# One bias tile with one-hot selectors, a new load order, and idle products at the planner's early gaps

## The chip, the cores and the metric

The kernel runs on one core of one Trainium2 chip. The metric is the device time of one execution in microseconds. A kernel's time is the median of its runs; a profiled execution is a run of its own, with its own time and a span (first to last instruction) that is a little shorter than that time.

## What is computed

The reference is one layer of an encoder trunk: 256 rows of 2048 values, all in 32-bit floats. A conditioning vector c gives six vectors of 2048 (shift, scale and gate for each of two sub-layers). The first sub-layer is windowed attention with 32 query heads and 8 key heads, the second a squared-ReLU MLP with 8192 hidden values:

```
mod = silu(c) @ mod_w + mod_b              # 2048 x 12288
sh_m, sc_m, g_m, sh_f, sc_f, g_f = split(mod, 6)
h = x * (1 + sc_m) + sh_m
y = attention(h @ w_qkv + b_qkv) @ w_o + b_o
x = layer_norm(alpha * x + (1 + g_m) * y)
h = x * (1 + sc_f) + sh_f
y = square(relu(h @ w1 + b1)) @ w2 + b2
out = layer_norm(alpha * x + (1 + g_f) * y)
```

Nearly all of the bytes are weights, each of which is read once: 288.54 MB in the profiled execution.

## The kernel before

**Split products.** TensorE (PE) multiplies in a reduced 32-bit form, so each operand is split into a high and a low part and a product is done as three: high by high, high by low, low by high (`mm3`, lines 893 to 898, which shows as L894, L895, L896). ScalarE (ACT) casts the high half of a weight (`Stream.half`, L614), and VectorE (DVE) subtracts it from the raw weight to get the low half (`Stream.low`, L572). One load is a raw tile of 128 x 2048 floats, 1 MB, and gives two halves of 128 x 1024. There are five high and five low half tiles, and eight raw tiles while the planned part lasts (five after it). All of these loads go out on the queue of SyncE (SP), in the order of one list, as raw tiles come free.

**Modulation.** The shift and scale of each 128-row chunk of the input come in one of two forms, chosen by `MIXP` (line 33): as a product on PE (`Mod.step`, L679; then a copy on ACT at L707, a product that turns it at L769, and an addition on DVE at L776), or as two columns on DVE (`Col.step`, L718), each of which multiplies a whole raw tile by the conditioning vector and sums it. Six of the 16 chunks are products. The column form needs the vector in all 128 partitions (`cb`); it is spread there by PE (`spread`, L972, whose stationary operand is one column read 128 times) and copied by ACT. The modulated input is then made on ACT (L924, L927) and DVE (L929). The first gate is four loads on PE and twelve columns on DVE.

**The gate row.** `Gate.spread` (line 810) turns the gate columns into a row: an addition on DVE (s1, L814), a product on PE (s2, L817), a copy on ACT and a store to DRAM from the queue of GpSimd (POOL) (s3, L820 and L821), and a read of that row into all 128 partitions, also from POOL's queue (s4, L824). The sums that use it are three operations on DVE for each column block and row tile: a product (tm, L1342), an addition (za, L1344), statistics (bn, L1346).

**The biases.** `bias_rows` (line 487) is called twice, for the attention's input bias (six rows of 512) and its output bias (four rows). Each call makes four tiles of 128 x 1024: the rows at partition 0 and 32, their split into a high and a low part, and a table of selectors in which each row of ones is written out 128 wide. ACT copies the selectors (L502), DVE splits the rows (L504, L505), and `add` (L508) multiplies a selector by the split rows to add one row to a bank.

**The order of the work.** From the start to about the eleventh weight of the MLP every engine's order is fixed by a planner, `flow_order` (line 122). `FLOW` (line 64) is the list of loads: "m" a modulation chunk (two loads), a number or a pair a weight of the attention's input product, "g" and "G" the gate's columns and products, "f" a column for the second modulation, "x" the rows of the input, ("o", c, j) a weight of the output product for column block c, "F" a weight of the MLP. `COST` (line 76) holds the planned duration of each kind of operation. The planner steps through time, takes for each engine what is ready, with ranks for ties, counts PSUM banks and raw tiles, and sorts all operations by planned start. The kernel then issues them in that order, and the helper `P` ties each instruction to the one before it on its engine, so an instruction that waits holds up all that stand behind it on its engine. After the planned part the MLP runs in four blocks in plain loops (L1503, L1505 and `mm3`).

**Idle products.** `idle(n)` (line 1005) issues n products of 128 x 512 into a bank that nobody reads, to keep PE's clock up. Before has 12 at the very start, 5 and 2 ahead of and between the first chunk's products, 8 behind its turn, and 18 ahead of the first layer norm.

Of the kernel before, what the change touches and what calls it, by code (L numbers as in the profile page):

```python
# [19 lines left out]
D = 2048  # L20
# [12 lines left out]
MIXP = tuple(int(k in (0, 1, 2, 4, 6, 15)) for k in range(16))  # L33
# [14 lines left out]
def mod_chunks():  # L48
# [8 lines left out]
    for which, p in (("m", GMP), ("f", 0)):  # L57
# [21 lines left out]
            s3=.2, s4=6.0, wm=1.4, v1=.3, v2=.25, v3=.43, n0=.46, n1=.74, fr=.3, fx=.4, fk=.45,  # L79
            fy=.6, ft=.82, fa=.46, fb=.46, fc=.36, w=1.44, ev=.5, ed=.6, i0=1.2, i1=.9, i2=.6, i3=.5, i4=.45, sv=1.0, sa=.96)  # L80
# [41 lines left out]
def flow_order():  # L122
# [4 lines left out]
    def op(key, eng, kind, after, rank, banks=(), frees=(), slot=False):  # L127
        ops[key] = eng, kind, list(after), rank, banks, frees, slot

    weights = [v[1] for v in loads if v[0] == "w"]  # L130
    tiles = max(i for i, v in enumerate(loads) if v[0] == "m")
    early = [v[1] for v in loads[:tiles] if v[0] == "w"]
    for k in range(NK):
        g0, g1 = ("g", k, 0), ("g", k, 1)
        if MIXP[k]:
            op(g0, "PE", "gP", [("m", k, 0)], 0, ("gv",) if k == 0 else (), (), True)
            op(g1, "PE", "gP", [("m", k, 1), g0], 0, (), (), True)
            op(("r", k), "ACT", "r", [g1], 0)
            op(("c", k), "PE", "c", [("r", k)], 0)
            op(("a", k), "DVE", "a", [("c", k)], 0, (), ("gv",) if not any(MIXP[k + 1:]) else ())  # L140
        else:
            for i, g in enumerate((g0, g1)):
                op(g, "DVE", "gD", [("m", k, i), ("cp", 3)], 2, (), (), True)
            op(("a", k), "DVE", "a", [g0, g1], 0)
        op(("H", k), "ACT", "H", [("a", k)], 0)
        op(("T", k), "ACT", "H", [("a", k)], 1)
        op(("S", k), "DVE", "S", [("H", k), ("T", k)], 0)
# [3 lines left out]
    for n in weights:  # L151
# [14 lines left out]
        for i in range(4):  # L166
# [37 lines left out]
            if kind == "u" and k == NK - 1 or kind == "l" and n[0] == 3 and i == 3:  # L204
                p = p if kind == "u" else n[1]
                op(("bq", p), "PE", "bq", [("u", n, i), ("sv", 0), ("sa", 0)], 1)
# [24 lines left out]
    for x in range(2):  # L231
        op(("sv", x), "DVE", "sv", [("i", 4)], 4)
        op(("sa", x), "ACT", "sa", [("i", 4)], 4)
# [132 lines left out]
    return [key for _, _, key in sorted(out)], loads  # L366
# [6 lines left out]
def hybrid_kernel(ctx: ExitStack, tc: tile.TileContext, a, out: bass.AP):  # L373
# [25 lines left out]
    def g4(dt=F32):  # L399
        return gen.tile([128, 1024], dt, tag="g4", name="g4")  # L400
# [86 lines left out]
    def bias_rows(src, n):  # L487


        m = n // 512  # L490
        raw, hl, one, sel = g4(), g4(F32R)[:, :512], g4(), g4(F32R)
        nc.gpsimd.memset(raw[:, :512], 0.0)
        nc.gpsimd.memset(one, 0.0)
        v = one[:, :m * 128].rearrange("p (m n) -> p m n", m=m)
        for p in (0, 32):
            nc.gpsimd.dma_start(raw[p:p + m, :512], src.rearrange("o (m n) -> (o m) n", m=m))
            nc.gpsimd.affine_select(out=v, in_=v, compare_op=OP.not_equal, fill=1.0, base=-p,
                                    pattern=[[-1, m], [0, 128]], channel_multiplier=1)

        def split(sels):  # L500
            if sels:
                P(nc.scalar.copy(sel, one))  # L502
            else:
                P(nc.vector.tensor_copy(hl, raw[:, :512]))  # L504
                P(nc.vector.tensor_sub(hl[32:32 + m], raw[32:32 + m, :512], f32(hl[32:32 + m])))  # L505

        def add(ps, c, stop=True):
            P(nc.tensor.matmul(ps, sel[:, c * 128:c * 128 + 128], hl, start=False, stop=stop))  # L508

        return split, add  # L510
# [330 lines left out]
    KEYS, LOADS = flow_order()  # L841
# [457 lines left out]
    split_bias, bq = bias_rows(a["bqkv"], QKV)  # L1299
    split_bo, bo = bias_rows(a["bo"], D)  # L1300
# [33 lines left out]
    def row_bias(c):  # L1334
        for t in range(NT):
            bo(out_of[c][0][t], c, False)
# [10 lines left out]

    for key in KEYS:
        op, *v = key
        if op == "g":  # L1350
            k, i = v
            S.take(load_of["m", k, i])
            if k == 0:
                idle((5, 2)[i])
# [8 lines left out]
        elif op == "c":  # L1363
            m_mix[v[0]].turned()
            if v[0] == 0:
                idle(8)
# [6 lines left out]
        elif op in ("sv", "sa"):  # L1373
            (split_bo if v[0] else split_bias)(op == "sa")
# [354 lines left out]
```

## Time and profile before

| what | before |
|---|---|
| median of 3 runs | 1078.09 us (1076.59 to 1078.45) |
| profiled execution | 1077.52 us |
| its span | 1075.7 us |
| PE busy | 1047.2 us, 97% |
| DVE busy | 821.4 us, 76% |
| ACT busy | 538.2 us, 50% |
| POOL busy | 22.3 us, 2% |
| moved by DMA | 291.63 MB, mean 271 GB/s |
| granted TensorE clock | 0.990 of full |

A line of a profile names the line of the kernel, the engine, the operation and the tiles as out<-in. Lines with "x" and a number group instructions. What stands in brackets at the end of a timeline's line is the time for which the engine had no work just before, and what ended that. PE's busy time is modelled (matmuls are pipelined), so a stop shows in the brackets, and a low clock shows only in the stretches' column of the granted clock. DVE and the DMA engines are the ones to watch up to about 420 us, PE alone behind that.

### The profile page before, as it was taken

The numbers are of one execution on the slowest core, as the hardware profiler recorded it, in microseconds if no ns is written. First come the engines' busy times: TensorE is split into PE (matmuls) and PEld (weight loads), VectorE is DVE, ScalarE is ACT, GpSimd is POOL, SyncE is SP. The second block draws the span as 40 slices with busy tenths as digits, with TensorE's granted clock in tenths as the row PEclk, the third lists the DMA queues.
The fourth block names the chain that finished last, engine by engine and source line by source line (L and its number), as shares of the span: only waits on it lengthen the run. The fifth ranks groups of instructions, "written<-read, shape, count | busy, mean of one in ns | idle before, by whom it ended". The sixth has DMA issues, their size and how long they took to land.

```text
span 1075.7 us, 15033 instructions
## 1 busy us (share of the span) xinstructions
PE 1047.2 (97%) x5896; PEld 875.8 (81%) x5896; DVE 821.4 (76%) x1139; ACT 538.2 (50%) x833; POOL 22.3 (2%) x45
## 2 busy tenths in 40 slices
PE   7999999999988999999999999999999999999997
PEld 5787776677767999988888888888888888888885
DVE  2679999899979999955787879656665557665795
ACT  3545359899414655733445543344543334554340
POOL 3000000000000000000000010000000000000000
PEclk8999999999989999999999999999999999999999
DMA  9999997668977998655778788756555555557522
GB/s 380 425 426 425 427 423 299 223 214 313 422 302 304 337 423 307 220 192 193 267 278 293 270 293 328 302 209 220 181 187 196 196 196 196 193 180 257 192 78 79
DMA packets 43463, 291.63 MB, mean 271 GB/s; under 512 B 4940, under 2 KB 5100, under 8 KB 9600
## 3 DMA queue, kind: packets, MB, share of 16 engines
q1 hardware_dynamic: 40256, 281.82, 69.1%
q0 software_dynamic: 2272, 7.40, 2.1%
q10 hardware_dynamic: 864, 1.45, 0.4%
q8 instruction: 46, 0.75, 0.3%
q14 instruction: 25, 0.20, 0.0%
HBM read 288.54 MB, written 2.11 MB: 270 GB/s over the span
## 4 chain that ended last, share of the span: by engine, by line
PE 76%; DVE 17%; ACT 3%; DMA 3%; issue 1%; SPq 0%; DVEq 0%; POOLq 0%; ACTq 0%
PE pa L1503 16%; PE pa L894 13%; PE pa L896 13%; PE pa L895 13%; PE pa L1505 9%; DVE raw L718 6%; DVE wl L572 5%; PE pa L1285 2%; PE pa L1283 2%; PE pa L1284 2%; DMA raw<-in_wqkv 1%; ACT g L1105 1%; PE pt L1111 1%; PE pa L1065 1%; DMA g<-rowm 1%
## 5 line engine op out<-in xcount | busy, mean ns | idle before, releaser
L572 DVE TENSOR_TENSOR wl<-raw,wh 128x1024 fp32r<-128x1024 f32 x332 | 402.1, 1222 | 191.6 <-ACT wh L603 175.6
L603 ACT CAST wh<-raw 128x1024 fp32r<-128x1024 f32 x226 | 237.9, 1053 | 317.6 <-PE pa L896 181.1
L894 PE MATMUL pa<-wh,g 128*128 128x512 f32 x816 | 323.8, 397 | 4.9 <-ACT wh L614 2.3
L895 PE MATMUL pa<-wl,g 128*128 128x512 f32 x816 | 320.8, 393 | 5.1 <-DVE wl L572 5.1
L896 PE MATMUL pa<-wh,g 128*128 128x512 f32 x816 | 320.4, 393 | 0.1
L1503 PE MATMUL pa<-g,wh 128*128 128x512 f32 x768 | 192.3, 392 | 0.0
L718 DVE CUSTOM_DVE_ANT_0 raw<-raw,cb 128x2048 f32<-128x2048 f32 x80 | 182.0, 2284 | 8.7 <-DMA raw<-in_mod 8.7
L894 PEld LDWEIGHTS pa<-wh,g 128*128 128x128 f32 x816 | 154.7, 190 | 40.7 <-issue 2.9
L895 PEld LDWEIGHTS pa<-wl,g 128*128 128x128 f32 x816 | 154.7, 190 | 37.4 <-DVE wl L572 6.6
L896 PEld LDWEIGHTS pa<-wh,g 128*128 128x128 f32 x816 | 154.7, 190 | 33.3 <-DVE g L929 0.7
L1503 PEld LDWEIGHTS pa<-g,wh 128*128 128x128 f32 x768 | 138.3, 189 | 25.1 <-ACT wh L603 0.2
L614 ACT CAST wh<-raw 128x1024 fp32r<-128x1024 f32 x106 | 109.1, 1051 | 95.4 <-PE pa L896 38.5
L1505 PEld LDWEIGHTS pa<-g,wl 128*128 128x128 f32 x768 | 104.8, 190 | 7.5
L1505 PE MATMUL pa<-g,wl 128*128 128x256 f32 x768 | 107.1, 282 | 0.0
L1284 PE MATMUL pa<-g,wh 128*128 128x256 f32 x256 | 72.5, 284 | 0.9 <-DVE g L1259 0.9
L1283 PE MATMUL pa<-g,wh 128*128 128x256 f32 x256 | 72.7, 285 | 0.6 <-DVE g L1293 0.3
L1285 PE MATMUL pa<-g,wl 128*128 128x256 f32 x256 | 72.5, 283 | 0.6 <-DVE wl L572 0.6
L1284 PEld LDWEIGHTS pa<-g,wh 128*128 128x128 f32 x256 | 49.1, 192 | 1.4 <-DVE g L1259 1.4
L1283 PEld LDWEIGHTS pa<-g,wh 128*128 128x128 f32 x256 | 48.9, 192 | 1.1 <-ACT g L1261 0.5
L1285 PEld LDWEIGHTS pa<-g,wl 128*128 128x128 f32 x256 | 49.1, 192 | 0.8 <-DVE wl L572 0.8
L1082 ACT ACTIVATE g<-g,nm 128x256 f32<-128x256 f32 x64 | 32.0, 508 | 0.9 <-DVE nm L1074 0.8
L1074 DVE CUSTOM_DVE_ANT_0 g<-pa,msk,nsnk 128x256 f32<-128x256 f32 x64 | 27.1, 476 | 2.0 <-PE pt L1111 1.1
(194 smaller groups left out, 703.9 us busy)
## 6 DMA issues: line engine op xcount, KB each, us to landing
raw<-in_mod SPq DMA_DIRECT2D x96, 1024.0 KB, 8.0
raw<-in_w SPq DMA_DIRECT2D x64, 1024.0 KB, 4.9
raw<-in_w1b SPq DMA_DIRECT2D x48, 1024.0 KB, 4.8
raw<-in_wqkv SPq DMA_DIRECT2D x24, 1024.0 KB, 10.8
raw<-in_wo SPq DMA_DIRECT2D x16, 1024.0 KB, 7.7
raw<-in_w1a SPq DMA_DIRECT2D x16, 1024.0 KB, 7.1
g<-in_x SPq DMA_DIRECT2D x4, 512.0 KB, 11.7
gb<-in_lnrow POOLq DMA_DIRECT2D x8, 256.0 KB, 5.6
```

What stands on the lines that cost most here:

```text
L572: self.pinned(nc.vector.tensor_sub(l, r, f32(self.hs[n])))
L603: self.last[n] = nc.scalar.copy(h, s)
L614: self.pinned(nc.scalar.copy(h, s))
L718: S.pinned(nc.vector.tensor_tensor_reduce(out=raw, in0=raw, in1=cb, scale=1.0, scalar=0.0, op0=OP.mult, op1=OP.add, accum_out=self.dst))
L894: S.pinned(nc.tensor.matmul(ps, xh, wh, start=start, stop=False))
L895: S.pinned(nc.tensor.matmul(ps, xh, wl, start=False, stop=False))
L896: S.prev = nc.tensor.matmul(ps, xl, wh, start=False, stop=stop)
L1283: S.pinned(nc.tensor.matmul(o, wh(w, 128), hh, start=new and fi + k == 0, stop=False))
L1284: S.pinned(nc.tensor.matmul(o, wh(w, 128), hl, start=False, stop=False))
L1285: S.pinned(nc.tensor.matmul(o, wl(w, 128), hh, start=False, stop=end and fi == 1 and k == 3))
L1503: nc.tensor.matmul(ps, wh(k, 128), ff_in(k), start=k == 0, stop=False)
L1505: nc.tensor.matmul(ps[:, :256], wl(k, 128), ff_in(k)[:, :256], start=False, stop=k == NK - 1)
```

## The change

Three things are changed, all in the planned part.

1. `bias_rows` is called once, with both biases. Their ten rows share one tile (at partitions 0 to 9 and again from 32 on). The selector of a row is one column of a small tile of 128 x 10, and `add` reads that column 128 times as its stationary operand. The split is one step on DVE (a copy of the small tile, then copy and subtraction of the rows); ACT has no part in it.
2. `FLOW` and `MIXP` are replaced. The product form goes to the chunks 0, 1, 2, 3, 10, 14 instead of 0, 1, 2, 4, 6, 15. The counts of all kinds of load are the same. In `COST`, s4 (the gate row's way back) is 15.0 instead of 6.0, and the two splits (sv, sa) become one sv of 1.2. The first product of a product-form chunk is planned behind the addition of the product-form chunk ahead of it.
3. The planner also returns `FILL`: for each operation of PE, how many idle products fit the gap that it plans ahead of it, at 0.3 us each. The kernel issues them as long as no spread and no weight of the pair form has come yet; the calls with 5, 2 and 8 are gone.

```
-MIXP = tuple(int(k in (0, 1, 2, 4, 6, 15)) for k in range(16))
+MIXP = tuple(int(k in (0, 1, 2, 3, 10, 14)) for k in range(16))
 FLOW = [
-    "m", "m", 0, 1, "m", 2, "m", "m", (0, 4), 3, (0, 3), (0, 5), "m", 4, "m", (1, 4), "m", "m", 5, (1, 3), "m", 6,
-    "m", (1, 5), 7, "m", (2, 3), 8, "m", (2, 5), 9, "m", 10, "m", "m", 11, "g", (3, 3), "f", "G", "f", (2, 4),
-    (3, 4), "G", (3, 5), "x", "g", "g", ("o", 0, 0), ("o", 0, 1), "g", ("o", 1, 1), "G", "f", ("o", 1, 2), "g", "g",
-    "f", "f", ("o", 0, 2), "g", ("o", 1, 0), "g", "g", "G", "g", "f", ("o", 1, 3), ("o", 0, 3), "f", "g", "g",
-    ("o", 2, 0), ("o", 3, 1), "f", ("o", 2, 2), "f", "f", ("o", 3, 0), "f", "f", ("o", 2, 3), ("o", 2, 1), "f", "f",
-    "f", "f", "f", ("o", 3, 3), ("o", 3, 2), "f", "f", "f", "f", "F", "F", "f", "F", "F", "f", "f", "F", "f", "F",
-    "F", "f", "f", "F", "f", "f", "f", "f", "F", "F", "F", "f", "F", "F",
+    "m", 0, "m", 1, "m", 2, (0, 5), "m", "m", (0, 3), "m", 3, "m", (0, 4), 4, (1, 5), "m", (1, 4), 5, "m", 6, "m",
+    (1, 3), 7, (2, 5), "m", "m", 8, (2, 3), "m", 9, "m", "m", 10, "m", 11, "g", (3, 3), "g", "G", "G", (2, 4),
+    (3, 4), "g", (3, 5), "g", ("o", 1, 0), "g", "g", "f", ("o", 0, 1), "f", "g", "f", "x", ("o", 1, 1), ("o", 0, 0),
+    "G", "f", "G", "g", "g", ("o", 1, 2), "f", "g", "g", "g", ("o", 0, 2), ("o", 1, 3), ("o", 0, 3), "f", "f",
+    ("o", 3, 3), ("o", 2, 1), ("o", 2, 3), "f", "f", "f", ("o", 3, 1), "f", "f", "f", ("o", 3, 2), "f", ("o", 3, 0),
+    "f", "f", "f", ("o", 2, 0), ("o", 2, 2), "f", "f", "f", "f", "F", "F", "f", "f", "F", "f", "F", "F", "f", "f",
+    "f", "F", "F", "f", "f", "f", "F", "f", "f", "F", "F", "F", "F", "F",
 ]
...
-            s3=.2, s4=6.0, wm=1.4, v1=.3, v2=.25, v3=.43, n0=.46, n1=.74, fr=.3, fx=.4, fk=.45,
+            s3=.2, s4=15.0, wm=1.4, v1=.3, v2=.25, v3=.43, n0=.46, n1=.74, fr=.3, fx=.4, fk=.45,
...
-            op(g0, "PE", "gP", [("m", k, 0)], 0, ("gv",) if k == 0 else (), (), True)
+            op(g0, "PE", "gP", [("m", k, 0)] + rowed, 0, () if rowed else ("gv",), (), True)
+            rowed = [("a", k)]
...
+    keys, fill, end = [], {}, 0.0
+    for t, _, key in sorted(out):
+        keys.append(key)
+        if ops[key][0] == "PE":
+            fill[key] = max(int((t - end - .2) / .3), 0) if end else 0
+            end = t + COST[ops[key][1]]
+    return keys, loads, fill
...
+    def bias_rows(srcs):
+
+        raw, hl = g4()[:, :512], g4(F32R)[:, :512]
+        m = [n // 512 for _, n in srcs]
+        one, pick = cst.tile([128, sum(m)], F32, name="one"), cst.tile([128, sum(m)], F32R, name="pick")
...
+        def split():
+            e = 32 + sum(m)
+            P(nc.vector.tensor_copy(pick, one))
+            P(nc.vector.tensor_copy(hl, raw))
+            P(nc.vector.tensor_sub(hl[32:e], raw[32:e], f32(hl[32:e])))
 
         def add(ps, c, stop=True):
-            P(nc.tensor.matmul(ps, sel[:, c * 128:c * 128 + 128], hl, start=False, stop=stop))
+            P(nc.tensor.matmul(ps, pick[:, c:c + 1].to_broadcast([128, 128]), hl, start=False, stop=stop))
...
+    free = True
     for key in KEYS:
         op, *v = key
+        free = free and op != "sp" and (op != "u" or type(v[0]) is int)
+        if free and FILL.get(key):
+            idle(FILL[key])
         if op == "g":
             k, i = v
             S.take(load_of["m", k, i])
-            if k == 0:
-                idle((5, 2)[i])
```

More of the change, by code (lines that the diff above doesn't have):

```diff
@@ L78 @@
             no=.4, pt=.43, pc=.48, va=1.9, oh=.48, ol=.6, tm=.6, za=.6, bn=.6, mr=.2, mt=.15, ma=.1, s1=.1, s2=.35,
-            s3=.2, s4=6.0, wm=1.4, v1=.3, v2=.25, v3=.43, n0=.46, n1=.74, fr=.3, fx=.4, fk=.45,
-            fy=.6, ft=.82, fa=.46, fb=.46, fc=.36, w=1.44, ev=.5, ed=.6, i0=1.2, i1=.9, i2=.6, i3=.5, i4=.45, sv=1.0, sa=.96)
+            s3=.2, s4=15.0, wm=1.4, v1=.3, v2=.25, v3=.43, n0=.46, n1=.74, fr=.3, fx=.4, fk=.45,
+            fy=.6, ft=.82, fa=.46, fb=.46, fc=.36, w=1.44, ev=.5, ed=.6, i0=1.2, i1=.9, i2=.6, i3=.5, i4=.45, sv=1.2)
 AFTER = dict(PE=.35, DVE=.2, ACT=.2, Q=0.0)
@@ L131, in flow_order @@
     tiles = max(i for i, v in enumerate(loads) if v[0] == "m")
+    rowed = []
     early = [v[1] for v in loads[:tiles] if v[0] == "w"]
@@ L205, in flow_order @@
                 p = p if kind == "u" else n[1]
-                op(("bq", p), "PE", "bq", [("u", n, i), ("sv", 0), ("sa", 0)], 1)
+                op(("bq", p), "PE", "bq", [("u", n, i), ("sv",)], 1)
                 d = done.setdefault(CORD[p], [])
@@ L215, in flow_order @@
             if out_of[c] == 0:
-                op(("bo", c), "PE", "bq", [("u", n, 3), ("sv", 1), ("sa", 1)], 3)
+                op(("bo", c), "PE", "bq", [("u", n, 3), ("sv",)], 3)
             out_of[c] += 1
@@ L230, in flow_order @@
         op(("i", x), "ACT" if x == 3 else "DVE", "i%d" % x, [("i", x - 1) if x else ("u", weights[0], 3)], 4)
-    for x in range(2):
-        op(("sv", x), "DVE", "sv", [("i", 4)], 4)
-        op(("sa", x), "ACT", "sa", [("i", 4)], 4)
+    op(("sv",), "DVE", "sv", [("i", 4)], 4)
     for v in loads:
@@ L365, in flow_order @@
         out.append((t, len(out), key))
-    return [key for _, _, key in sorted(out)], loads
+    keys, fill, end = [], {}, 0.0
[5 more added lines that the diff above has]
+    return keys, loads, fill
 ORDER_ONLY = mybir.DependencyInfo(mybir.DependencyClass.NoSync, mybir.DependencyReason.DATA)
@@ L484, in rotary_tables @@
         yield
[L487 to L492, printed above, removed]
+    def bias_rows(srcs):
+        raw, hl = g4()[:, :512], g4(F32R)[:, :512]
+        m = [n // 512 for _, n in srcs]
+        one, pick = cst.tile([128, sum(m)], F32, name="one"), cst.tile([128, sum(m)], F32R, name="pick")
+        nc.gpsimd.memset(raw, 0.0)
         nc.gpsimd.memset(one, 0.0)
-        v = one[:, :m * 128].rearrange("p (m n) -> p m n", m=m)
         for p in (0, 32):
[L496 to L505, printed above, removed]
+            for (src, _), i, k in zip(srcs, (0, m[0]), m):
+                nc.gpsimd.dma_start(raw[p + i:p + i + k], src.rearrange("o (m n) -> (o m) n", m=k))
+            nc.gpsimd.affine_select(out=one, in_=one, compare_op=OP.not_equal, fill=1.0, base=-p,
+                                    pattern=[[-1, sum(m)]], channel_multiplier=1)
+        def split():
[3 more added lines that the diff above has]
+            P(nc.vector.tensor_sub(hl[32:e], raw[32:e], f32(hl[32:e])))
         def add(ps, c, stop=True):
-            P(nc.tensor.matmul(ps, sel[:, c * 128:c * 128 + 128], hl, start=False, stop=stop))
+            P(nc.tensor.matmul(ps, pick[:, c:c + 1].to_broadcast([128, 128]), hl, start=False, stop=stop))
         return split, add
@@ L839, in hybrid_kernel @@
     m_gf = Gate("f", 0, gateb[:, 1])
-    KEYS, LOADS = flow_order()
+    KEYS, LOADS, FILL = flow_order()
     load_of = {}
@@ L1298, in hybrid_kernel @@
     load_x(0)
-    split_bias, bq = bias_rows(a["bqkv"], QKV)
-    split_bo, bo = bias_rows(a["bo"], D)
+    split_bias, bq = bias_rows(((a["bqkv"], QKV), (a["bo"], D)))
     msk = masks()
@@ L1335, in row_bias @@
         for t in range(NT):
-            bo(out_of[c][0][t], c, False)
+            bq(out_of[c][0][t], QKV // 512 + c, False)
     def gated_sum(op, c, t):
@@ L1364, in hybrid_kernel @@
             m_mix[v[0]].turned()
-            if v[0] == 0:
-                idle(8)
         elif op == "a":
@@ L1372, in hybrid_kernel @@
             next(rotary)
-        elif op in ("sv", "sa"):
-            (split_bo if v[0] else split_bias)(op == "sa")
+        elif op == "sv":
+            split_bias()
         elif op == "h":
```

## The prediction

> **What bounds the kernel now.** I read the page first, then stretches of the span, then the waits, then the chain and the timeline around the longest wait.
>
> ```profile
> span 1075.7 us, 15033 instructions
> ...
> L572 DVE TENSOR_TENSOR wl<-raw,wh 128x1024 fp32r<-128x1024 f32 x332 | 402.1, 1222 | 191.6 <-ACT wh L603 175.6
> ...
> L718 DVE CUSTOM_DVE_ANT_0 raw<-raw,cb 128x2048 f32<-128x2048 f32 x80 | 182.0, 2284 | 8.7 <-DMA raw<-in_mod 8.7
> ```
>
> The profiled execution took 1077.52 us, 1.8 us more than its span; the median of the three runs is 1078.09, that is 0.57 us more than this execution. L572 makes the low half of a weight (1.22 us for each 128x1024 half); L718 makes one column of the modulation from one load (2.28 us). Both run on VectorE (DVE) and follow the planner's order. Next, chosen stretches; the columns are the stretch and its length, busy time and count of TensorE (PE), of its weight loads, of DVE, ScalarE (ACT) and GpSimd (POOL), then the granted clock, the DMA share and GB/s.
>
> ```profile
> 19.00:26.00 7.00, 6.32 (x16) 4.76 (x17) 5.06 (x5) 3.93 (x6) 0.00 (x0) 0.52 1.03 434
> 46.20:50.00 3.80, 3.73 (x9) 2.56 (x10) 2.50 (x4) 3.80 (x6) 0.00 (x0) 0.55 1.01 425
> 80.00:140.00 60.00, 58.48 (x256) 47.40 (x255) 59.77 (x69) 27.69 (x34) 0.00 (x0) 1.00 1.01 426
> 160.00:260.00 100.00, 96.19 (x657) 67.60 (x656) 94.49 (x241) 93.10 (x259) 0.00 (x0) 1.00 0.67 254
> 296.00:304.00 8.00, 7.89 (x35) 6.19 (x33) 2.73 (x5) 2.41 (x3) 0.00 (x0) 1.00 1.01 422
> 303.90:307.80 3.90, 0.01 (x1) 0.01 (x1) 3.83 (x7) 0.85 (x1) 0.00 (x0) 0.77 0.15 63
> 307.80:312.80 5.00, 5.00 (x12) 3.94 (x13) 5.00 (x6) 0.00 (x0) 0.00 (x0) 0.50 0.79 279
> 320.00:340.00 20.00, 20.00 (x90) 16.56 (x89) 19.86 (x23) 4.88 (x5) 0.00 (x0) 1.00 0.98 396
> 460.00:1040.00 580.00, 580.00 (x2913) 493.95 (x2912) 392.96 (x462) 259.04 (x310) 8.01 (x15) 1.00 0.64 227
> ```
>
> From 460 to 1040 us PE has no free time and no other engine is near full. The diff leaves that stretch as it is, so whatever the planned part (up to some 420 us) gains or loses goes to the end one for one. In the planned part there are several limits: the DMA engines and DVE both full from 80 to 140, PE, DVE and ACT all over 93% from 160 to 260. The weak place is at 296 to 313: DVE works 2.73 of 8 us, then PE stands for 3.9 us, and then PE has half its clock for 5 us. The waits of DVE say why; the columns are the total, the number of times and the longest.
>
> ```profile
> DVE tmp L1342 <- DMA g<-rowm: 5.8, 1, 5.8
> DVE modm L776 <- PE gv L769: 5.4, 3, 4.7
> ```
>
> The chain and DVE's timeline show the way of the gate row: from the copy on ACT, through DRAM and back in 128 copies, to the first product with it.
>
> ```profile
> 286.88 0.26 ACT grow L820
> ...
> 287.42 5.19 DMA rowm<-grow
> ...
> 293.19 7.98 DMA g<-rowm
> ```
>
> ```profile
> 295.31 0.08 DVE L718 DVE_READ_ACCUMULATOR2_ANT modf<- 128x1 f32 x1
> 301.20 0.69 DVE L1342 TENSOR_TENSOR tmp<-pa,g 128x512 f32<-128x512 f32 x1 [5.80 <-DMA g<-rowm]
> ...
> 306.52 4.62 DVE L572 TENSOR_TENSOR wl<-raw,wh 128x1024 fp32r<-128x1024 f32 x4
> ```
>
> From the end of the copy (287.14) to the first product that uses the row (301.20) it is 14.06 us. The planner of before counts 6.0 for this (s4), and so puts the products eight microseconds too early in DVE's queue. Behind them stand four halves of weights (306.52), and PE runs dry at 303.9 because they are late.
>
> **The change, part by part.**
>
> *The gate row at 15 (s4).* Planned at 15, the products of L1342 stand behind 15 us of other DVE work, 0.9 us more than the way took. Low halves and columns are there to fill it: the load list has three output weights behind the last gate column, and modulation loads after them. PE needs no bank from these products meanwhile: four column blocks of the output product take eight banks, and before had already begun its third block ahead of them. The order search also puts the last gate column at load 82 instead of 87, five loads earlier. What PE loses here now is 3.90 us standing and 5.00 us at clock 0.50, so 3.9 + 2.5 = 6.4 us; what DVE loses is 5.80. From 320 to 340 DVE is busy 19.86 of 20, so PE cannot gain more than DVE gives: I take 5.8, with ends 0 (the wait comes elsewhere) and 6.4.
>
> Here the Trainium skill speaks against the change. "DMA: Bandwidth & Descriptors", section "Anatomy of one DMA — SWDGE (gpsimd) path", fits a GpSimd-issued DMA as 2.0 us plus its bytes at 436 GB/s; for the row of 8 KB and then 1 MB this estimate is 2.0 + 4.4 = 6.4 us, which would make the old 6.0 right, leave nothing to gain in this term, and put the sum at 1075.1 instead of 1069.3 for the profiled execution. The rows differ from it: 5.19 and 7.98 us, with the other loads holding the DMA engines at a share of 1.01. The wait of 5.80 is measured, so the rows decide.
>
> *The load order of the first 52 loads and the forms (MIXP).* Product form on PE stays at six of 16 chunks, so DVE keeps 20 column loads of 2.28 us and the DMA engines the same bytes. Three product chunks move: 4, 6 and 15 become columns, 3, 10 and 14 products. The first weight now comes after one modulation chunk, not two. PE's early losses are here:
>
> ```profile
> 19.16 0.74 PE L894 MATMUL pa<-wh,g 128*128 128x512 f32 x1 [2.28 <-ACT wh L614]
> ...
> 46.14 0.50 PE L894 MATMUL pa<-wh,g 128*128 128x512 f32 x1 [1.79 <-ACT g L924]
> ...
> 150.40 0.62 PE L508 MATMUL pa<-g,g 128*128 128x512 f32 x2
> ```
>
> Two stops of 2.28 and 1.79 us, each followed by a cold stretch (7.0 us at 0.52 costs 3.4, 3.8 at 0.55 costs 1.7): 9.2 us in all. Not all of it can come back. The DMA engines must bring 52 loads of 1.049 MB and 2.1 MB of the input, 56.6 MB, at 426 GB/s: 133 us; half a cast, 1.2 us of low half and 24 products at 0.222 us (90 in 20 us) then end no earlier than about 141, against 150.40 for the bias product that follows the last chunk. That room is more than DVE can use, which is full from 80 to 140 (59.77 of 60). What DVE visibly wastes ahead of that is the one wait of 4.7 us for a product-form chunk queued behind weights on PE (chunk 6, now a column). I take half of it, 2.4 us, because another chunk may come late instead; ends 0 and 5.8 (the 4.7 and the bias work below), and a loss is the rival below.
>
> *Idle products.* Before has 5, 2 and 8 of them at the first chunk; now the planner's gaps are filled, 0.3 us counted for each where a warm one takes 0.222 and a cold one twice that. A gap of 3 us gets nine, which take 2.0 us warm and 4.0 us cold, so a cold fill can end 1.0 us late. They stop at the first spread of the conditioning vector or the first quarter, so the stop at 44 us is not of the kind that they cover. PE waits for loads there anyway: 0, ends minus 1 and plus 1 us.
>
> *One bias tile.* Removed: one split on DVE and both ACT copies of selectors; added: a copy of 10 columns.
>
> ```profile
> L972 PEld LDWEIGHTS pa<-ident,cact x32: 185/190/333, 24.9 to 32.8; 128*128 128x128 f32 x32
> ```
>
> ```profile
> L508 PEld LDWEIGHTS pa<-g,g x20: 186/188/192, 150.2 to 300.3; 128*128 128x128 f32 x20
> ```
>
> ```profile
> 41.78 0.43 DVE L504 CAST g<-g 128x512 fp32r<-128x512 f32 x1
> 42.25 0.68 DVE L505 TENSOR_TENSOR g<-g,g 4x512 fp32r<-4x512 f32 x1
> ```
>
> DVE saves 1.1 us less one small copy, near 42 us, where it is not full; it is inside the end of 5.8 above and counts 0 alone. The selector is now one column read 128 times, as L972 already loads its weight: 190 ns against 188 for the stored selector, over 20 products, 0. POOL's DMAs stay four and its fills get smaller, all before 10 us: 0. The input rows (x) load nine places later; they are first used behind the products with the gate row: 0. With more tiles free and the row of gv waited for by name, no wait is added that before did not have.
>
> *The rest of the order (160 to 420 us).* The same operations in a new sequence. DVE's idle time from 160 to 260 is 5.5 us; taking a third of it away, or adding as much, gives ends of minus 2 and plus 2. Later, the eighth weight of the next layer moves from load 123 to 126: three loads at 2.46 us, 7.4 us of lead lost where DMA is nearly full; at worst a stop of about 2 us and a cold stretch like that after 46 us, 1.7: plus 4. I take 0.
>
> **Sum:** 1077.52 - 5.8 - 2.4 = 1069.3 for the profiled execution; with 0.57 for the median, 1069.9 us.
>
> **The rivals.**
>
> *Gate row alone.* The start stays bound by the DMA engines (share 1.01 from 80 to 140) and gives nothing: 1078.09 - 5.8 = 1072.3. For it: PE and DVE both trail the loads. Against it: the 4.7 us wait.
>
> *The wait returns.* The row's way runs beside the loads; DVE no longer stalls, so raw tiles are freed and loads press on. Each microsecond beyond 15 is again a wait of DVE, and at 20.8 the 5.8 are back; if the start gives nothing either, 1076 to 1078. Against it: the share was 1.01 already while the row was under way. This is also the case in which the change doesn't do what it says.
>
> *Slower: the last modulation chunk as a column.* Chunk 15 was a product, and is now two columns at loads 50 and 51, just ahead of the last weight.
>
> ```profile
> 119.42 7.82 SPq L556 DMA_DIRECT2D raw<-in_mod  x4
> ```
>
> ```profile
> 138.56 2.28 DVE L718 CUSTOM_DVE_ANT_0 raw<-raw,cb 128x2048 f32<-128x2048 f32 x1
> ...
> 144.42 0.43 DVE L929 TENSOR_TENSOR g<-xm,g 128x256 fp32r<-128x256 f32 x1 [1.16 <-ACT xm L927]
> ```
>
> ```profile
> raw<-in_mod SPq DMA_DIRECT2D x4, 1024.0 KB, 8.7
> ```
>
> Chunk 14's first load was issued at 119.42 and landed 8.7 us later, at 128.1; DVE took it at 138.56, 10.4 us behind. Chunk 15 lands two loads (4.9 us) later, 133.0. With the same backlog: 143.4, two columns to 148.0, 1.7 for the rest as from 143.1 to 144.85, then 18 products (4.0) to 153.7: 3.3 us later than 150.40. PE has nothing else meanwhile, since the next chunk needs the same columns, and starts cold: 2.5 as after 307.8. Plus 5.8 is just the gate row's gain, so 10.4 us of backlog is where it decides; at 14 the total is 1078.1 + 3.6 = 1081.7. Against it: chunks 10 and 14 are now products, which gives DVE four loads (9.8 us) without columns, where before had none between loads 23 and 49.
>
> **How the numbers follow.** Forecast 0.48; gate row alone 0.22; wait returns 0.15; last chunk late 0.15. About 0.2% (2.2 us) is what a measurement of this kernel can tell from no change. The first two are faster, with 0.02 of the third: 0.72; the third otherwise the same: 0.13; the fourth slower: 0.15. The range reaches down by the upper ends (6.4, 5.8 and 2 from 1078.1: 1063.9, rounded to 1063.5) and up to 1077.5, which leaves out the slower rival and the worst of the third.
>
> **What would show it.** Right: no wait of DVE on g<-rowm over 1 us; no stop of PE over 1.5 us and no cold stretch between 160 and the layer norm; the output product's last chunk 5 to 9 us earlier; the bias product of the first stage at 147 to 149. Wrong: the bias product after 151 with a stop ahead of it; DVE again idle on the row; a new stop with a clock near 0.5 in the next layer's first weights; or a stretch from 460 to 1040 that is not full.

## The result and the profile after

| | before | after |
|---|---|---|
| median, runs side by side | 1077.34 us (4 runs, 1076.42 to 1078.45) | 1064.96 us (4 runs, 1064.95 to 1066.41) |
| ratio, 95% interval | 1 | 0.9888 [0.9871, 0.9905] |
| profiled execution, its span | 1077.52, 1075.7 us | 1064.97, 1063.2 us |

The kernel is 12.4 us faster. The page of after, its first lines:

```profile
span 1063.2 us, 15010 instructions
...
PE 1042.3 (98%) x5894; PEld 873.4 (82%) x5894; DVE 820.2 (77%) x1138; ACT 535.5 (50%) x831; POOL 17.4 (2%) x41
```

PE has 4.9 us less busy time than the 1047.2 of before (PE at half clock is busy for longer with the same work); the other 7.6 us of the span were free time of PE. To place them I cut the span at four instructions that both kernels have. The rows of a source line give a group's durations, then its first and last start; before, then after:

```profile
L1130 PE MATMUL pa<-g,g x128: 379/379/431, 181.8 to 271.6; 128*64 128x256 f32 x128
...
L1247 PE MATMUL pt<-ident,g x32: 270/295/476, 344.9 to 388.3; 128*128 128x128 f32 x32
...
L1503 PE MATMUL pa<-g,wh x768: 389/389/497, 535.0 to 976.5; 128*128 128x512 f32 x192
```

```profile
L513 PEld LDWEIGHTS pa<-g,pick x20: 185/188/192, 144.8 to 291.6; 128*128 128x128 f32 x20
L513 PE MATMUL pa<-g,pick x20: 390/397/501, 145.1 to 291.8; 128*128 128x512 f32 x20
...
L1135 PE MATMUL pa<-g,g x128: 379/379/430, 173.9 to 264.3; 128*64 128x256 f32 x128
...
L1252 PE MATMUL pt<-ident,g x32: 272/273/421, 330.1 to 371.2; 128*128 128x128 f32 x32
...
L1507 PE MATMUL pa<-g,wh x768: 389/389/497, 522.4 to 963.9; 128*128 128x512 f32 x192
```

**Start** runs up to the first bias product (150.4 before, by the prediction's row; 145.1 after), **attention** from there to the last product with the values (L1130, now L1135), **gate row** from there to the first transpose behind the layer norm (L1247, now L1252), **MLP start** from there to the first product of the plain loops (L1503, now L1507). The change of each: start -5.3, attention -2.0 (121.2 to 119.2), gate row -7.5 (73.3 to 65.8), MLP start +2.3 (190.0 to 192.3); together -12.5, the whole change of the span. The same stretches as in the prediction, for after (times shifted with the work):

```profile
19.00:26.00 7.00, 6.00 (x63) 4.86 (x62) 4.24 (x11) 4.06 (x6) 0.00 (x0) 1.00 1.02 425
46.20:50.00 3.80, 3.03 (x13) 2.17 (x12) 3.80 (x5) 2.27 (x4) 0.00 (x0) 1.00 1.03 425
100.00:140.00 40.00, 40.00 (x272) 32.20 (x265) 33.67 (x41) 15.40 (x22) 0.00 (x0) 1.00 1.01 421
160.00:260.00 100.00, 99.03 (x651) 72.36 (x650) 98.63 (x249) 97.29 (x270) 0.00 (x0) 1.00 0.80 298
287.00:303.00 16.00, 16.00 (x72) 13.17 (x72) 15.86 (x19) 5.27 (x5) 0.00 (x0) 1.00 0.98 390
386.00:388.40 2.40, 1.01 (x6) 0.81 (x7) 1.79 (x3) 1.89 (x3) 0.00 (x0) 0.99 1.01 423
388.40:391.80 3.40, 3.40 (x18) 3.40 (x18) 3.40 (x5) 2.68 (x3) 0.00 (x0) 0.50 0.83 296
447.00:1027.00 580.00, 580.00 (x2913) 493.95 (x2912) 392.55 (x462) 259.47 (x310) 7.99 (x15) 1.00 0.64 227
```

The clock is 1.00 where before had 0.52 and 0.55. In the attention PE is busy 99.03 of 100 instead of 96.19. Through the sums with the gate row (287 to 303) PE never stops. In the plain loops PE's figures are unchanged to the hundredth. New is a weak place at 386. The waits of DVE, and its timeline with POOL's and ACT's around the row:

```profile
DVE modm L781 <- PE gv L774: 10.4, 3, 5.0
DVE raw L723 <- DMA raw<-in_mod: 8.4, 6, 3.6
```

```profile
270.68 0.26 ACT L825 COPY grow<-pt 16x128 f32<-16x128 f32 x1 [0.63 <-PE pt L822]
...
277.29 1.09 POOL L829 DMA_DIRECT2D g<-rowm  x2 [5.54 <-DMA rowm<-grow]
...
286.39 0.68 DVE L1346 TENSOR_TENSOR tmp<-pa,g 128x512 f32<-128x512 f32 x1
...
385.54 1.99 ACT L619 CAST wh<-raw 128x1024 fp32r<-128x1024 f32 x2 [6.27 <-DMA raw<-in_w1a]
...
386.63 0.39 PE L1288 MATMUL pa<-g,wh 128*128 128x256 f32 x1 [0.73 <-ACT wh L619]
...
387.89 0.38 PE L1290 MATMUL pa<-g,wl 128*128 128x256 f32 x1 [0.75 <-DVE wl L577]
```

No wait on g<-rowm is left: the first product with the row has no bracket, 15.45 us after ACT's copy ended (286.39 less 270.94). At 386 ACT stands 6.27 us for the load of the ninth MLP weight, PE stops twice for 0.7 us and then works at half clock. The wait for product-form chunks (modm<-gv), of which I meant to win half, has grown from 5.4 to 10.4 us; that for column loads (8.4) is what it was (8.7).

### The profile page after: what moved, and what is told of

It reads as the page before. It is cut to its first block, busy times and chain, and to the rows that moved or that the text cites. A ratio compares the mean times of both kernels' runs of the same rounds, so it can differ in the third digit from the quotient of the medians.

```text
span 1063.2 us, 15010 instructions
## 1 busy us (share of the span) xinstructions
PE 1042.3 (98%) x5894; PEld 873.4 (82%) x5894; DVE 820.2 (77%) x1138; ACT 535.5 (50%) x831; POOL 17.4 (2%) x41
## 4 chain that ended last, share of the span: by engine, by line
PE 70%; DVE 18%; DMA 8%; issue 2%; ACT 1%; DVEq 0%; ACTq 0%; SPq 0%
PE pa L1507 17%; PE pa L899 13%; PE pa L900 13%; PE pa L901 13%; PE pa L1509 9%; DVE raw L723 7%; DVE wl L577 5%; DMA raw<-in_mod 3%; DVE g L1079 2%; DMA raw<-in_wqkv 2%; PE pa L1289 2%; PE pa L1290 2%; PE pa L1288 2%; DMA raw<-in_w1a 1%; DVE g L1033 1%
## 5 line engine op out<-in xcount | busy, mean ns | idle before, releaser
L577 DVE TENSOR_TENSOR wl<-raw,wh 128x1024 fp32r<-128x1024 f32 x332 | 401.4, 1221 | 189.9 <-ACT wh L608 175.7
L1507 PE MATMUL pa<-g,wh 128*128 128x512 f32 x768 | 192.3, 392 | 0.0
L1507 PEld LDWEIGHTS pa<-g,wh 128*128 128x128 f32 x768 | 138.3, 189 | 25.1 <-ACT wh L608 0.2
L1288 PE MATMUL pa<-g,wh 128*128 128x256 f32 x256 | 74.1, 291 | 0.7 <-ACT wh L619 0.7
L1289 PE MATMUL pa<-g,wh 128*128 128x256 f32 x256 | 74.3, 291 | 0.4 <-DVE g L1264 0.4
L1288 PEld LDWEIGHTS pa<-g,wh 128*128 128x128 f32 x256 | 50.7, 199 | 0.9 <-ACT wh L619 0.9
L1289 PEld LDWEIGHTS pa<-g,wh 128*128 128x128 f32 x256 | 50.6, 198 | 1.1 <-DVE g L1264 1.0
L1110 ACT ACTIVATE g<-g,rs 128x256 f32<-128x256 f32 x64 | 27.6, 502 | 1.7 <-DVE rs L1105 1.4
```

What stands on the lines that cost most here:

```text
L577: self.pinned(nc.vector.tensor_sub(l, r, f32(self.hs[n])))
L1288: S.pinned(nc.tensor.matmul(o, wh(w, 128), hh, start=new and fi + k == 0, stop=False))
L1289: S.pinned(nc.tensor.matmul(o, wh(w, 128), hl, start=False, stop=False))
L1507: nc.tensor.matmul(ps, wh(k, 128), ff_in(k), start=k == 0, stop=False)
```

## The experiments

"b_" kernels are before with one part of the change, "a_" kernels are after with one part undone or altered. Ratios are against before, run beside them. The median of before was 1078.55 us beside b_s4, a_s4_6, a_nofill and b_front, 1078.22 beside b_s4_wo8, b_rear, b_bias and a_tail, 1077.75 beside the other four. The stretches are those above, each from one execution; I read nothing from differences under 1 us.

| kernel | median us | ratio [95%] | start | attention | gate row | MLP start |
|---|---|---|---|---|---|---|
| before | 1077.34 | 1 | 150.4 | 121.2 | 73.3 | 190.0 |
| after | 1064.96 | 0.9888 [0.9871, 0.9905] | 145.1 | 119.2 | 65.8 | 192.3 |
| b_s4 | 1084.91 | 1.0062 [1.0041, 1.0082] | 149.9 | 121.2 | 80.8 | 190.1 |
| a_s4_6 | 1073.02 | 0.9955 [0.9939, 0.9971] | 145.7 | 118.2 | 73.9 | 191.7 |
| b_s4_wo8 | 1075.73 | 0.9975 [0.9962, 0.9987] | 150.4 | 121.2 | 71.3 | 189.9 |
| b_rear | 1071.27 | 0.9947 [0.9930, 0.9963] | 149.9 | 120.9 | 67.6 | 190.3 |
| b_front | 1073.87 | 0.9962 [0.9951, 0.9974] | 144.5 | 119.7 | 75.8 | 193.0 |
| b_warm | 1073.70 | 0.9967 [0.9956, 0.9979] | 146.6 | 121.2 | 73.4 | 189.4 |
| a_nofill | 1065.26 | 0.9881 [0.9866, 0.9896] | 145.6 | 118.3 | 66.4 | 192.6 |
| b_bias | 1070.68 | 0.9936 [0.9921, 0.9951] | 147.1 | 116.5 | 73.7 | 190.5 |
| b_hold | 1077.54 | 1.0001 [0.9986, 1.0015] | 147.1 | 121.3 | 73.7 | 191.5 |
| a_oldbias | 1065.41 | 0.9891 [0.9871, 0.9911] | 144.0 | 121.7 | 65.9 | 191.8 |
| a_tail | 1062.82 | 0.9865 [0.9850, 0.9880] | 145.5 | 118.4 | 66.2 | 189.1 |
| a_tail_warm | 1064.36 | 0.9879 [0.9860, 0.9897] | 145.6 | 119.1 | 65.9 | 191.1 |

### The gate row: number or list?

**b_s4**, before with the new number alone.

```
-            s3=.2, s4=6.0, wm=1.4, ...
+            s3=.2, s4=15.0, wm=1.4, ...
```

> The kernel before with one number changed: the gate row's way is planned at 15.0 instead of 6.0; list of loads, forms, bias tiles and idle products as before. Theory A (the prediction's gate term): the number alone takes the 5.8 us wait of VectorE on the row away, the stop of 3.9 us and the cold stretch go with it, and the time is about 1077.3 - 5.8 = 1071.5 us. Theory B: the old list holds too little work behind its last gate column (load 87) to fill 15 us, so the wait only changes place; the layer norm begins where it did and the time is 1076 to 1078 us.

It is slower by 0.6%, which neither theory has. Timeline of b_s4, DVE and PE:

```profile
302.89 2.29 DVE L718 CUSTOM_DVE_ANT_0 raw<-raw,cb 128x2048 f32<-128x2048 f32 x1 [3.59 <-DMA raw<-in_mod]
...
307.87 0.69 DVE L1342 TENSOR_TENSOR tmp<-pa,g 128x512 f32<-128x512 f32 x1
...
313.18 3.49 DVE L572 TENSOR_TENSOR wl<-raw,wh 128x1024 fp32r<-128x1024 f32 x3
...
314.46 0.79 PE L895 MATMUL pa<-wl,g 128*128 128x512 f32 x1 [11.08 <-DVE wl L572]
```

DVE no longer waits for the row, but it waits 3.59 us for a load of a column instead, and the low halves still stand behind the sums (313.18 behind 307.87). Those sums are now later, so PE stops for 11.08 us where it stopped for 3.90.

**a_s4_6**, after with the old number.

```
-            s3=.2, s4=15.0, wm=1.4, ...
+            s3=.2, s4=6.0, wm=1.4, ...
```

> The changed kernel with the gate row's way planned at 6.0 again; all else as after the change. Theory A: the number decides where the products with the row stand in VectorE's queue, so VectorE waits about 8 us on the row again, TensorE stops behind it, and the time rises by 5 to 8 us, to 1070 to 1073 us. Theory B: the new list, with the last gate column five loads earlier, covers the way by itself; the time stays at 1065 to 1066 us.

The waits of a_s4_6:

```profile
DVE tmp L1346 <- DMA g<-rowm: 6.8, 1, 6.8
...
PE pa L900 <- DVE wl L577: 7.1, 3, 6.1
```

DVE waits 6.8 us on the row again and PE 6.1 us for a low half. The gate-row stretch is back at 73.9: in this list the number is worth 8 us, while in the list of before it costs 7.5 (b_s4). Neither the list nor the number alone shortens that stretch.

**b_s4_wo8**, why the halves stand behind the sums. The planner lets the output product hold only four banks, two column blocks of two row tiles; the sums free them.

```
-BANKS = dict(sum=6, gv=1, q=1, lt=2, wo=4, pm=1, ...)
+BANKS = dict(sum=6, gv=1, q=1, lt=2, wo=8, pm=1, ...)
...
+            s3=.2, s4=15.0, wm=1.4, ...
```

> The kernel before with the gate row planned at 15.0 and the planner's count of banks for the output product raised from 4 to 8; list, forms, bias tiles and idle products as before. With 15.0 alone VectorE no longer waited on the row, but the planner had put four low halves behind the sums, and TensorE stopped for 11.1 us. Theory A: the count of 4 did that (the planner may not begin a third column block until a sum is planned, so the halves for it are planned behind the sums); with 8 the halves come first, no stop over 1.5 us at 300 us, and the time is 1078.5 - 6 = 1071 to 1073 us. Theory B: the old list itself is too short behind its last gate column; the stop stays over 3 us and the time is 1077 us or more.

The waits of PE in b_s4_wo8:

```profile
PE pt L1247 <- DVE g L1191: 3.7, 1, 3.7
PE pa L895 <- DVE wl L572: 2.4, 3, 1.3
```

The stop of 11.08 us is gone (1.3 us is the longest for a low half), so the cap did put the halves behind the sums. But the gate-row stretch is only 2.0 us shorter than before: 3.7 us now go ahead of the first transpose of the layer norm. The time, 1075.73, lies between the ranges of the two theories.

**b_rear**, before with the new list behind the last weight of the input product, and 15.

```
-... 11, "g", (3, 3), "f", "G", "f", (2, 4), (3, 4), "G", (3, 5), "x", "g", "g", ("o", 0, 0), ...
+... 11, "g", (3, 3), "g", "G", "G", (2, 4), (3, 4), "g", (3, 5), "g", ("o", 1, 0), "g", "g", ...
...
+            s3=.2, s4=15.0, wm=1.4, ...
```

> The kernel before with the new list behind the last weight of the input product and 15.0 for the gate row; first 52 loads, forms, bias tiles and idle products as before. The new first part alone gave -4.7 us of -13. Theory A (two separate gains that add): the rest, about 8 us, is here: 1069.5 to 1071.5 us, with no stop near the gate row. Theory B (the new second part needs the earlier start): 1074 us or more.

The stretch is 67.6: 5.7 us of the 7.5 come with list and number together, without the new start, the bias tile or the idle products.

### The start: loads, clock or idle products?

**b_front**, before with the new forms and the new list up to the last weight of the input product.

```
-MIXP = tuple(int(k in (0, 1, 2, 4, 6, 15)) for k in range(16))
+MIXP = tuple(int(k in (0, 1, 2, 3, 10, 14)) for k in range(16))
...
-    "m", "m", 0, 1, "m", 2, "m", "m", (0, 4), 3, (0, 3), (0, 5), "m", 4, ...
+    "m", 0, "m", 1, "m", 2, (0, 5), "m", "m", (0, 3), "m", 3, "m", (0, 4), 4, ...
```

> The kernel before with the new list up to the last weight of the input product (52 loads) and the new forms; the rest of the list, the 6.0 for the gate row, both bias tiles and the idle products 5, 2, 8 as before. Theory A (the start's gain is TensorE's: first weight 3.3 us earlier, no cold stretch at 19 and at 46 us): the bias product of the first stage at 145 to 146 instead of 150.4, and about 5 us of it stay to the end: 1071.5 to 1073 us. Theory B (the prediction's 2.4 us, VectorE's wait for a late product chunk): the bias product at 147.5 to 148.5, time 1074.5 to 1075.5 us. Theory C (the middle swallows it): the bias product early, but the layer norm where it was, 1077 us.

The stretches of b_front:

```profile
19.00:26.00 7.00, 7.00 (x80) 5.61 (x71) 4.40 (x12) 4.33 (x7) 0.00 (x0) 1.00 1.03 428
46.20:50.00 3.80, 2.87 (x13) 2.06 (x12) 3.80 (x5) 2.29 (x4) 0.00 (x0) 1.00 1.00 418
```

The bias product starts at 144.5 (-5.9), and the half clock at 19 and 46 us is gone. The list and the forms alone make the start. Of the 5.9 us, 2.5 are lost again at the gate row (75.8) and 3.0 at the MLP's start; that the rest of the old list does not fit there is my reading, not shown. The time, 1073.87, lies between the ranges of theories A and B. (The profiled execution was 1.7 us above the median of this kernel, so the late stretches show rather too much.)

**b_warm**, before with idle products ahead of the first weight product and of the tenth unit of the first stage, nothing else.

```
+            if v == [0, 0]:
+                idle(9)
+            if v == [2, 1]:
+                idle(8)
```

> The kernel before with 9 idle products ahead of the first weight product (the stop of 2.28 us) and 8 ahead of the tenth unit (the stop of 1.79 us at 44 us); nothing else. Theory A (half the start's loss is the clock): the stretches at half clock at 19 and 46 us go, the first bias product comes 2 to 5 us before 150.4, and the time falls by as much: 1073.5 to 1076.5 us. Theory B (loads or VectorE set the pace in the first 150 us): the clock is full, the bias product within 1 us of 150.4, time 1077.3 to 1079 us.

The stretches of b_warm:

```profile
19.00:26.00 7.00, 5.98 (x32) 4.84 (x32) 5.06 (x5) 4.70 (x7) 0.00 (x0) 1.00 1.03 434
46.20:50.00 3.80, 3.80 (x18) 3.17 (x17) 3.42 (x5) 3.70 (x4) 0.00 (x0) 1.00 1.00 423
```

Same loads, same DVE work, only the clock at 1.00: the start is 3.8 us shorter, and the gain stays to the end (ratio 0.9967). So for these 3.8 us PE's pace set the start, not DVE and not the loads. DVE is still full from 80 to 140 (59.24 of 60 us, before 59.77), and yet the bias product comes earlier.

**a_nofill**, after without its idle products.

```
-        if free and FILL.get(key):
-            idle(FILL[key])
```

> The changed kernel without the 13 idle products of the planned gaps (the 12 at the very start and the 18 ahead of the layer norm stay). Theory A (idle products keep the clock): TensorE goes cold in the first 20 us, a stretch at half clock of 3.4 to 6.8 us shows by 15 to 27 us, and the bias product of the first stage comes 1.5 to 3.5 us after 145.1; time 1066.5 to 1068.5 us. Theory B (the order keeps TensorE fed and the loads set the pace): at most a short cold stretch that is caught up with; the bias product at 145 to 146 and the time within 0.7 us of 1065.0.

The stretches of a_nofill:

```profile
12.40:19.30 6.90, 4.18 (x38) 3.34 (x38) 2.79 (x3) 2.98 (x4) 0.00 (x0) 0.51 1.00 416
19.00:26.00 7.00, 7.00 (x81) 5.74 (x83) 3.47 (x9) 4.03 (x7) 0.00 (x0) 0.98 1.01 416
```

Half clock from 12 to 19 us costs nothing: PE is busy for 4.18 of 6.90 us there, has room to be slow in, and the start is 145.6 against 145.1. The time is that of after. Here the idle products are worth nothing. (The equal times alone would not show it, since a_nofill has 3.4 us less of half clock at the layer norm than after; the start does.)

### The bias tile

**b_bias**, before with `bias_rows` of after and the one split where the first split was.

```
-    split_bias, bq = bias_rows(a["bqkv"], QKV)
-    split_bo, bo = bias_rows(a["bo"], D)
+    split_bias, bq = bias_rows(((a["bqkv"], QKV), (a["bo"], D)))
...
+            P(nc.tensor.matmul(ps, pick[:, c:c + 1].to_broadcast([128, 128]), hl, start=False, stop=stop))
...
+            if key == ("sv", 0):
+                split_bias()
```

> The kernel before with one bias tile and one-hot columns read 128 times, its split issued where the first split was; planner's order, list and idle products as before. The prediction says 0: the work saved on VectorE, ScalarE and GpSimd is not on the path. 1077.5 to 1079 us. Rival: the column read 128 times as a weight or the one split costs time in the 20 bias products: over 1080 us; or the freed tiles and engine time are worth 1 to 2 us: under 1077 us.

I had put it at nothing, and it gives 7.5 us. Two things happen. DVE's timeline, before and then b_bias (with the next product of PE):

```profile
42.96 2.29 DVE L718 CUSTOM_DVE_ANT_0 raw<-raw,cb 128x2048 f32<-128x2048 f32 x1
```

```profile
40.34 0.68 DVE L504 TENSOR_TENSOR g<-g,g 10x512 fp32r<-10x512 f32 x1
41.05 2.29 DVE L717 CUSTOM_DVE_ANT_0 raw<-raw,cb 128x2048 f32<-128x2048 f32 x1
...
44.24 0.50 PE L893 MATMUL pa<-wh,g 128*128 128x512 f32 x1 [0.68 <-ACT g L923]
```

The second split of before (41.78 to 42.93, in the prediction's rows) stood right ahead of the column that PE's stop of 1.79 us waited for. Without it the column starts 1.9 us earlier, the stop is 0.68, and the half clock behind it is gone. The half clock at 19 us is shorter too (mean clock 0.76 from 19 to 26 us, before 0.52), for a reason that I did not find. Together the start gives -3.3. And the attention takes 116.5 us instead of 121.2, with PE's busy time in the stretch from 160 to 260:

```profile
160.00:260.00 100.00, 98.72 (x682) 72.29 (x683) 98.80 (x248) 98.39 (x272) 0.00 (x0) 1.00 0.77 290
```

**b_hold**, b_bias with three of the general tiles that it frees held until the bias products that had used them. It adds three copies of one column on DVE.

```
+        pads.extend(g4() for _ in range(3))
+        for v in pads:
+            nc.gpsimd.memset(v[:, :16], 0.0)
...
+            for _ in range(n):
+                P(nc.vector.tensor_copy(sink, pads.pop()[:, :1]))
...
+        hold("bq", 6, 1)
...
+        hold("bo", 4, 2)
```

> The kernel with one bias tile alone (b_bias, 1070.7 us) plus three tiles of 128 x 1024 that are filled in part at the start and held, as before held its selectors and second split: one until the last input bias product, two until the last output bias product; each is read once by a copy of one column. Nothing else changes. Theory A (shortage of the 20 general tiles in the attention): the start stays early (first bias product at 147), the attention is slow again, and the time is 1074.5 to 1076 us. Theory B (the 7.5 us come from the work saved on VectorE and ScalarE near 40 us alone, and carry on): 1070 to 1071.5 us.

```profile
160.00:260.00 100.00, 96.12 (x657) 67.89 (x656) 94.45 (x242) 93.75 (x263) 0.00 (x0) 1.00 0.73 274
```

The stretch of b_hold is that of before again (96.12 against 96.19 of 100), the attention takes 121.3, and the start keeps its 147.1. So the attention's part of the gain is the tiles: before, an operation waits for a free one of the twenty. Which one, the waits of ACT in the attention show, before and then b_bias (for the same copy):

```profile
ACT g L1120 <- PE pa L1065: 3.5, 2, 2.2
...
ACT g L1120 <- PE pa L1130: 1.4, 1, 1.4
```

```profile
ACT g L1119 <- PE pt L1110: 0.2, 1, 0.2
```

L1120 copies the turned attention weights out of a bank, and each pair of copies takes a new general tile (`PT[n] = g4()`). The products that end its waits, those for the scores (L1065) and those with the values (L1130), do not make what it copies; they read general tiles. It stands 2.17, 1.31 and 1.35 us in before, 4.8 in all, and 2.12, 1.31 and 1.34 us in b_hold; in b_bias it never stands over 0.3 us. That is the size of the attention's part, 4.7 us. Up to the last input bias product b_hold holds four tiles for the biases, as before does, and behind it one more than before; the three waits and the whole loss lie ahead of it (from the first to the last input bias pair it is 63.1 us in before and b_hold, 58.0 in b_bias).

The median of b_hold is that of before, more than theory A has, although the start stays 3.3 us earlier in the profiled execution. That execution was 1.3 us under the median, and its MLP's start is 1.0 us longer than b_bias's, where the three copies may have a part.

**a_oldbias**, after with the two bias tiles, selectors and splits of before (b_bias's edit in reverse, with both splits one behind the other).

> The changed kernel with the two bias tiles, their stored selectors and their two splits of before, issued one behind the other where the one split stands; order, list and idle products as after the change. Theory A (the tiles that the change frees matter in the new order too): 5 to 8 us slower, 1070 to 1073 us, the loss between the first bias product and the last attention product. Theory B (in the new order the splits and tiles are hidden, as the prediction had it): 1065 to 1066.5 us.

The time is that of after (0.9891 against 0.9888): the attention takes 2.5 us longer, with a stop of PE of 1.74 us and 3.4 us of half clock at 208 to 214 us, and the start 1.1 us less. In the new order the bias tile is worth nothing that can be measured.

### The new weak places

**a_tail**, after with the loads behind the last weight of the output product in the order of before.

```
-    "f", "f", "f", "f", "F", "F", "f", "f", "F", "f", "F", "F", "f", "f", "f", "F", "F", "f", "f", "f", "F", ...
+    "f", "f", "f", "f", "F", "F", "f", "F", "F", "f", "f", "F", "f", "F", "F", "f", "f", "F", "f", "f", "f", ...
```

> The changed kernel with the loads behind the last output weight in the order of before (the eighth weight of the next layer at 123 instead of 126, the ninth at 128 instead of 129). In the changed kernel TensorE stops twice for 0.75 us at 386 to 388 us at its ninth weight, which waits for its load, and has half its clock until 391.8. Theory A: the list put that weight too late; the stop and the cold stretch go and the time falls by 2 to 3 us to 1062 to 1063 us. Theory B: the loads of this stage come as fast as they can (DMA share 0.97 to 1.00 at 340 to 380 us), so that being early only means waiting there; the stop stays at 1 us or more and the time within 0.7 us of 1065.

The stretches of a_tail:

```profile
386.00:388.40 2.40, 2.40 (x22) 2.40 (x22) 2.40 (x3) 1.65 (x2) 0.00 (x0) 1.00 0.99 413
388.40:391.80 3.40, 3.40 (x30) 3.40 (x30) 3.40 (x4) 1.05 (x1) 0.00 (x0) 1.00 1.01 422
```

No stop and no half clock there; PE starts 52 products in these 5.8 us, after 24. The MLP's start is 3.2 us shorter, the median 2.1 us lower. This is the fastest version: 0.9865 of before. Its interval overlaps that of after, and the two were not run side by side; the place of the gain is plain in the stretches, its size is not settled.

**a_tail_warm**, a_tail with more idle products at the layer norm, to shorten the half clock there.

```
-NORM = 18
+NORM = 24
...
+                if g + kp + i == 0 and t:
+                    idle(8, oT[last_wo[2]][0])
```

> The version with the load tail of before (a_tail, 1062.8 us), with 24 instead of 18 idle products ahead of the first layer norm and 8 more between its first two transposes, where TensorE stands for 1.5 and 2.0 us and then has half its clock for 6.8 us. Theory A (the clock follows the idle products): the stretch at half clock behind the layer norm gets shorter by at least 3.4 us, and the time falls by 1.5 to 3 us: 1060 to 1061.5 us. Theory B (VectorE or the loads set the pace behind the layer norm, or the transposes keep the clock low): within 0.7 us of 1062.8.

The stretch behind the layer norm, a_tail and then a_tail_warm:

```profile
333.00:345.00 12.00, 11.56 (x73) 10.85 (x71) 11.70 (x18) 10.98 (x21) 0.00 (x0) 0.72 0.66 231
```

```profile
333.00:345.00 12.00, 9.73 (x65) 9.03 (x66) 11.68 (x18) 11.49 (x21) 0.00 (x0) 0.86 0.57 190
```

The half clock lasts 3.4 us instead of 6.8, and the kernel is not faster (1064.36 us, outside both ranges). DVE is busy 11.7 of the 12 us in both, so it may set the pace there. But the eight idle products also put the second run of transposes back, from 332.37 to 333.59, and this run does not separate the two: why nothing is gained stays open.

## Why the prediction was right, and where its steps failed

**Gate row, -5.8 forecast, -7.5 found.** The mechanism holds with list and number together: no wait on the row, no stop, full clock. The step that failed is the one that carried the number: the 15 us would be filled because "PE needs no bank from these products meanwhile: four column blocks take eight banks". I counted eight, but the planner's cap for the output product is four; with the old list it puts the low halves behind the later sums, and the number costs 6.4 us (1084.91 less 1078.55, b_s4). I took the number as the cause and the list as its help; each needs the other (a_s4_6, b_rear). The size, 5.8, rested on "PE cannot gain more than DVE gives", and its upper end, 6.4, on what PE lost by the stop and the clock, both read from the old order. The stretch gained 7.5, more than either. In the new order DVE works 15.86 of 16 us from 287 to 303; that this moved the bound is my reading, and what the last 1.1 us are was not taken apart.

The way of the row was 14.06 us before. In after the first half of the row landed 14.71 us behind the copy, at 285.65, and its first product began 0.74 us later, so 15.0 leaves little. The prediction took the 7.98 us of its row for the whole 1 MB; the row comes back as two reads of 512 KB (g<-rowm x2), and 7.98 us is the first. The second landed at 304.89 in before, 289.55 in after, and no sum of the first four needs it.

The Trainium skill's estimate ("DMA: Bandwidth & Descriptors", section "Anatomy of one DMA — SWDGE (gpsimd) path") made 6.0 right. With the first read at 512 KB, the same fit gives an estimate of 2.0 us for the store and 3.2 us for the read, 5.2 us in all, still further from the 14.06 measured. The trace does not agree, and the measurement decides: a_s4_6 puts what planning 6.0 costs in this list at 8 us.

**Start, -2.4 forecast, -5.3 found.** This term was mis-sized because its step failed: "That room is more than DVE can use, which is full from 80 to 140". A full DVE there did not bound the start: in b_warm it is as full (59.24 of 60), and the start is 3.8 us earlier. Nor need it be full there: with the new list it works 33.86 of 40 from 100 to 140 (b_front; after 33.67), while in after its wait for product chunks doubled. What set 3.8 us of the start was PE's two stretches at half clock, which I priced at 5.1 us and did not put into the sum (b_warm); the list gives 5.9 (b_front), and the rest of that is not taken apart.

**Idle products, 0:** right, for the reason given (a_nofill).

**One bias tile, 0:** right in the new order (a_oldbias), but by luck, for the reason was wrong. I looked at DVE's share near 42 us ("where it is not full") and not at what stood next in its queue: the column on which PE's stop hung. And "with more tiles free ... no wait is added" did not ask which wait it would take away: 4.7 us of the attention in the old order, ACT's copy at L1120 (b_hold).

**Rest of the order, 0:** -2.0 in the attention and +2.3 at the MLP's start, each inside its ends. The -2.0 is not the order's alone: with the old bias tiles in the same order the attention takes 121.7 us (a_oldbias). The loss is the kind foreseen, a stop and a half clock at a weight that moved back, but at the ninth weight and not the eighth; a_tail takes it away.

**Signs.** No wait on the row, and no stop over 1.5 us or half clock between 160 and the layer norm: as said. The bias product came ahead of the 147 to 149 named, for the start's reason. The output product's last chunk came 15.2 us earlier (its last product at 324.5, before 339.7), not 5 to 9. Of the signs of a wrong forecast one is there, a half clock in the next layer's first weights, and it is the +2.3.

**Rivals.** Gate row alone: refuted, the start gave 5.3. The wait returns: refuted, no wait on g<-rowm. The last chunk late: refuted, the bias product came 5.3 us earlier, not 3.3 later.

**Sum.** The gains of the parts don't add up. The two halves of the list do: b_front -4.68 and b_rear -6.95 make -11.6, a_oldbias, which has both and the idle products, has -12.3. But b_bias alone has -7.5 and adds nothing to them, since the lists take the same losses away: b_front has no half clock at 46 us, and in b_rear the copy of the turned weights never waits for a tile. That the sum fell inside its range owes something to luck: both its terms were too small, and the term put at nothing for a wrong reason happened to add nothing. The forecast was 1069.9 against 1078.09, a ratio of 0.9924; measured 0.9888.

## What to carry to other kernels

A planner's duration and the list that was searched with it are one thing: correct a number without a new search, and the queue behind it can get worse than the wait it cures. A free instruction is judged by what stands right behind it in its engine's queue, and a freed tile by who waits for one, not by the engine's share of the stretch. Look at the clock before the loads: a stop of under 2 us may cost as much again at half clock, though not everywhere (from 12 to 19 us in a_nofill it cost nothing, and at the layer norm in a_tail_warm halving it gained nothing).

## What the runs showed of the hardware

- Half clock came in stretches of 3.41 or 6.83 us, once of 10.24 us (b_s4, behind the stop of 11.08 us). The length of the stop ahead of it did not decide alone. It followed stops of 2.28 and 1.79 us (before), of 1.74 us (at 208 us, a_oldbias) and a pair of 0.73 and 0.75 us at 386 (after); single stops of 1.21 us (at 14 us, after) and 1.67 us (at 14 us, a_oldbias) had none behind them. The Trainium skill ("TensorE: Matmul & The Clock Gate", section "HAM oscillation — how this bites in real kernels") gives the rule as no idle gap over about 3.4 us. The length of the stretches agrees with its figure, and the 3.90 us of before and the 11.08 of b_s4 fit the rule; the stops of 0.73 to 2.28 us were all shorter than it.
- One column read 128 times as the stationary operand loads in 188 ns, the same as the stored selector's 188.
- POOL's store of 8 KB took 5.19 us before, with the other loads under way (POOL waited 5.54 for it in after): two thirds of the 7.98 us of the first read of 512 KB behind it, which moves 64 times as much.
